# A batched matmul on one core: from a scheduled tile kernel to hand-written engine programs with a TensorE loop

## Chip, core, metric

One core of a Trainium2 chip. The metric is the device time of a whole execution in microseconds, as the median of several executions. The span, which the profile uses, runs from the first to the last instruction and is some 1.8 us shorter than the device time. Runs carry a state: fast, or slow when a run is over 1.5% above the fastest of the same kernel.

## The reference

```python
def setup_inputs():
    batch, m, k, n = 16, 512, 768, 1024
    # x: (batch, k, m), y: (batch, k, n), both float32, random

def reference(x, y):
    return np.einsum('bkm,bkn->bmn', x, y).astype(np.float32)
```

Sixteen products of a 512x768 by a 768x1024 matrix. The inputs are 75.5 MB, the output 33.55 MB, all in HBM and all float32. The kernels multiply in bf16.

## The kernel before

For each batch, SyncE issues the load of x, the load of y and, four batches late, the store of a result, all on one queue. VectorE casts x in one piece and y in two halves of K. TensorE runs four groups (mo) of 12 matmuls, and ScalarE copies each finished group out of PSUM, where the matmuls write (`ps<-y_sb,x_sb` in the page, x768). The tile framework puts in the waits. Only in the last batch is y loaded in two halves, and K is the outer loop there.

```python
    with tc.manual_schedule():
        for b in range(B):
            xs = xs_pool.tile([P, KT, M], FP32, name="xs")       # 2 buffers
            ys = ys_pool.tile([P, KT, N], FP32, name="ys")       # 2 buffers
            halves = 2 if b == B - 1 else 1
            nc.sync.dma_start(xs[:], x_v[b])
            for h in range(halves):
                ks = slice(h * KT // halves, (h + 1) * KT // halves)
                nc.sync.dma_start(ys[:, ks], y_v[b, :, ks])
            if b >= LAG:                                         # LAG = 4
                store(b - LAG)
            # ... cut: tiles x_sb, y_sb, o_sb
            nc.vector.tensor_copy(x_sb[:], xs[:])
            for h in range(2):
                ks = slice(h * KH, (h + 1) * KH)
                nc.vector.tensor_copy(y_sb[:, ks], ys[:, ks])
            for h in range(halves):
                for mo in range(MT):
                    # ... cut: matmuls over nt and this half's kt into ps[mo]
                    if h == halves - 1:
                        nc.scalar.copy(o_sb[:, mo]..., ps[mo][:])
        for b in sorted(o_tiles):
            store(b)
```

## Time and profile before

| | before |
|---|---|
| device time, us (3 runs) | 262.01 (261.9 to 262.17) |
| span of the profiled run, us | 260.4 |
| TensorE, VectorE, ScalarE busy | 73%, 32%, 25% |
| DMA queue, share of 16 engines' span | 98.5% |
| first load issued, us | 0.73 |
| last store issued and landed, us | 246.0 and 259.5 |

Two more views matter for what follows. The first is SyncE's timeline of the kernel before, with start, duration, line and the transfer:

```profile
0.73 0.38 SPq L59 DMA_DIRECT2D xs<-in_x_dram  x1
...
9.10 0.33 SPq L59 DMA_DIRECT2D xs<-in_x_dram  x1
18.07 0.33 SPq L62 DMA_DIRECT2D ys<-in_y_dram  x1
```

x of batch 2 is issued at 9.10, when the cast of x(0) is over (7.31 + 1.76 = 9.07); y of batch 2 waits until 18.07, for the casts of y(0) (14.62 + 3.43 = 18.05). The second is the view of the output tile. Its last line gives the times from issue to landing of the 16 stores, and the last store is the shortest of them:

```profile
DMA to landing us min/median/max: 13.5/32.6/36.5
```

It is issued at 246.02, when the last copy ends (244.99 + 1.01).

### The profile page before, as it was taken

To read this page: it belongs to the slowest core of one execution; us is meant where nothing else is said; L and a number is where in the kernel's file an instruction comes from. 1 tells how busy PE (TensorE), PEld (TensorE's weight loads), DVE (VectorE), ACT (ScalarE), POOL (GpSimd) and SP (SyncE) were. 2 spreads that over 40 slices of the span, in tenths; PEclk is the share of its full clock that TensorE was granted. 3 is DMA by queue.
4 is the path that set the end of the run, shared out by engine and by line. 5 is a ranking of instruction groups with operands and counts; after the bars stand their busy time and mean duration, and the time that the engine had idled before them with its cause. 6 is when DMAs were issued, how large, how long until landed. Compare 5 with 4: busy or idle time off the path is not lost.

```text
span 260.4 us, 1815 instructions
## 1 busy us (share of the span) xinstructions
PE 189.9 (73%) x768; PEld 89.1 (34%) x768; DVE 83.1 (32%) x48; ACT 66.2 (25%) x65; POOL 0.2 (0%) x4
## 2 busy tenths in 40 slices
PE   0049999897939949598495956939789597899600
PEld 0014555453513514244142422514325233355200
DVE  0271734525222252322524214252132522252000
ACT  1003343433321313314033330412404114131600
POOL 0000000000000000000000000000000000000000
PEclk9999999999986997979899997997959869799955
DMA  7999999999999999999999999999999999999995
GB/s 276 430 427 425 451 420 436 423 386 421 439 428 430 422 433 445 418 435 422 435 436 414 452 405 448 429 415 452 413 434 426 421 447 416 427 437 422 428 435 214
DMA packets 7065, 109.18 MB, mean 419 GB/s; under 512 B 784, under 2 KB 784, under 8 KB 784
## 3 DMA queue, kind: packets, MB, share of 16 engines
q1 hardware_dynamic: 7056, 109.06, 98.5%
q8 instruction: 6, 0.10, 0.1%
q14 instruction: 3, 0.02, 0.0%
HBM read 75.50 MB, written 33.55 MB: 419 GB/s over the span
## 4 chain that ended last, share of the span: by engine, by line
DMA 74%; DVE 11%; PE 8%; ACT 0%; issue 0%; SPq 0%; DVEq 0%
DMA ys<-in_y_dram 74%; DVE y_sb L70 11%; PE ps L83 8%; ACT o_sb L88 0%; SPq L59 0%; DVEq L70 0%
## 5 line engine op out<-in xcount | busy, mean ns | idle before, releaser
L83 PE MATMUL ps<-y_sb,x_sb 128*128 128x512 bf16 x768 | 189.9, 410 | 55.1 <-DVE y_sb L70 55.1
L83 PEld LDWEIGHTS <-x_sb 128*128 128x128 bf16 x768 | 89.1, 118 | 155.3 <-issue 44.6
L88 ACT COPY o_sb<-ps 128x1024 f32<-128x1024 f32 x64 | 64.9, 1014 | 179.1 <-PE ps L83 179.1
L70 DVE CAST y_sb<-ys 128x3072 bf16<-128x3072 f32 x32 | 55.0, 1757 | 87.6 <-DMA ys<-in_y_dram 87.6
L67 DVE CAST x_sb<-xs 128x3072 bf16<-128x3072 f32 x16 | 28.2, 1760 | 66.4 <-DMA xs<-in_x_dram 65.6
L88 ACT ACT_TABLE_LOAD x1 | 1.3, 1283 | 0.7 <-PEq L105 0.7
L105 POOL MEMSET const-bfloat16-1.0<- 128x1 bf16 x1 | 0.1, 101 | 0.0
L105 POOL MEMSET const-uint8-127<- 128x1 uint8 x1 | 0.1, 101 | 0.0
L105 POOL MEMSET const-float32-0.0<- 128x1 f32 x1 | 0.1, 98 | 0.2 <-issue 0.2
L105 POOL MEMSET const-float32-1.0<- 128x1 f32 x1 | 0.1, 98 | 0.0
## 6 DMA issues: line engine op xcount, KB each, us to landing
ys<-in_y_dram SPq DMA_DIRECT2D x15, 3072.0 KB, 28.1
out_dram<-o_sb SPq DMA_DIRECT2D x16, 2048.0 KB, 32.6
xs<-in_x_dram SPq DMA_DIRECT2D x16, 1536.0 KB, 29.7
ys<-in_y_dram SPq DMA_DIRECT2D x2, 1536.0 KB, 26.1
```

The lines of the kernel that those rows point to most:

```text
L67: nc.vector.tensor_copy(x_sb[:], xs[:])
L70: nc.vector.tensor_copy(y_sb[:, ks], ys[:, ks])
L83: nc.tensor.matmul(ps[mo][:, nt], x_w[:, kt, mo], y_sb[:, kt, nt * NF:(nt + 1) * NF], start=(kt == 0), stop=(kt == KT - 1))
L88: nc.scalar.copy(o_sb[:, mo].rearrange("p (t f) -> p t f", f=NF), ps[mo][:])
L105: nc = _bacc.Bacc("TRN2", target_bir_lowering=False, num_devices=1)
```

## The change

Intent: replace the framework's schedule by one program per engine, with semaphores chosen by hand. TensorE's program becomes a loop over pairs of batches. It takes credits ("ready" from the casts, "room" from the copies) and subtracts them as it takes them, so that the loop body can be the same each time. Three things change with it. x is issued only after all casts of the batch two earlier. The last batch is like the others. The whole stands in a critical section with its own entry and exit.

```diff
-            halves = 2 if b == B - 1 else 1
-            nc.sync.dma_start(xs[:], x_v[b])
-            ... y in one or two loads
+    ctx.enter_context(tc.tile_critical())
+    ... buffers and semaphores by name; block = ec(nc.Block())
+    @block.sync
+    def _(sync):
+        for b in range(B):
+            if b >= 2:
+                sync.wait_ge(cast, b - 1)
+            sync.dma_start(xs[i][:], x_v[b]).then_inc(sx[i], 16)
+            sync.dma_start(ys[i][:], y_v[b]).then_inc(sy[i], 16)
+            if b >= LAG:
+                store(b - LAG)
+    @block.vector
+    ... waits on sx, sy; each cast adds 1 to ready; a drain adds 1 to cast
+    def batch(tensor, i, first):
+        tensor.wait_ge(ready, 2).then_inc(ready, -2)
+        for mo in range(MT):
+            tensor.wait_ge(room, 1).then_inc(room, -1)
+            for nt in range(NT):
+                for kt in range(KT):
+                    if mo == 0 and nt == 0 and kt == KH:
+                        tensor.wait_ge(ready, 1).then_inc(ready, -1)
+                    mm = nc.tensor.matmul(...)
+            mm.then_inc(groups, 1)
+    @block.tensor
+    def _(tensor):
+        with tensor.Fori(0, B // 2):
+            batch(tensor, 0, False)
+            batch(tensor, 1, False)
+    @block.scalar
+    ... waits on groups; each copy adds 1 to room; a drain adds 1 to outs
```

More of the change, by code (lines that the diff above doesn't have):

```diff
@@ L37 @@
     o_v = out.rearrange("b (p mo) n -> b p mo n", mo=MT)
-    xs_pool = ctx.enter_context(tc.tile_pool(name="xs_pool", bufs=2))
-    ys_pool = ctx.enter_context(tc.tile_pool(name="ys_pool", bufs=2))
-    x_pool = ctx.enter_context(tc.tile_pool(name="x_pool", bufs=2))
-    y_pool = ctx.enter_context(tc.tile_pool(name="y_pool", bufs=2))
-    o_pool = ctx.enter_context(tc.tile_pool(name="o_pool", bufs=5))
-    psum = ctx.enter_context(tc.tile_pool(name="psum", bufs=4, space=bass.MemoryType.PSUM))
@@ L45 @@
     LAG = 4
+    NO = 5
     KH = KT // 2
-    o_tiles = {}
-    def store(b):
-        o_sb = o_tiles.pop(b)
-        nc.sync.dma_start(o_v[b], o_sb[:])
-    with tc.manual_schedule():
-        for b in range(B):
-            xs = xs_pool.tile([P, KT, M], FP32, name="xs")
-            ys = ys_pool.tile([P, KT, N], FP32, name="ys")
-            halves = 2 if b == B - 1 else 1
-            nc.sync.dma_start(xs[:], x_v[b])
-            for h in range(halves):
-                ks = slice(h * KT // halves, (h + 1) * KT // halves)
-                nc.sync.dma_start(ys[:, ks], y_v[b, :, ks])
+    GP = NT * NF
@@ new lines @@
+    ctx.enter_context(tc.tile_critical())
+    ec = ctx.enter_context
+    xs = [ec(nc.sbuf_tensor(f"xs{i}", [P, KT, M], FP32)) for i in range(2)]
+    ys = [ec(nc.sbuf_tensor(f"ys{i}", [P, KT, N], FP32)) for i in range(2)]
+    xb = [ec(nc.sbuf_tensor(f"xb{i}", [P, KT, M], BF16)) for i in range(2)]
+    yb = [ec(nc.sbuf_tensor(f"yb{i}", [P, KT, N], BF16)) for i in range(2)]
+    ob = [ec(nc.sbuf_tensor(f"ob{i}", [P, MT, N], FP32)) for i in range(NO)]
+    ps = [ec(nc.psum_tensor(f"ps{i}", [P, NT, NF], FP32)) for i in range(MT)]
@@ new lines, with store @@
+    sx = [ec(nc.semaphore(f"sx{i}")) for i in range(2)]
+    sy = [ec(nc.semaphore(f"sy{i}")) for i in range(2)]
+    so = [ec(nc.semaphore(f"so{i}")) for i in range(NO)]
+    cast = ec(nc.semaphore("cast"))
+    ready = ec(nc.semaphore("ready"))
+    room = ec(nc.semaphore("room"))
+    groups = ec(nc.semaphore("groups"))
+    outs = ec(nc.semaphore("outs"))
+    block = ec(nc.Block())
+    @block.sync
+    def _(sync):
+        def store(b):
+            sync.wait_ge(outs, b + 1)
+            sync.dma_start(o_v[b], ob[b % NO][:]).then_inc(so[b % NO], 16)
+        for b in range(B):
+            i = b % 2
+            if b >= 2:
+                sync.wait_ge(cast, b - 1)
+            sync.dma_start(xs[i][:], x_v[b]).then_inc(sx[i], 16)
+            sync.dma_start(ys[i][:], y_v[b]).then_inc(sy[i], 16)
@@ L63, with _ @@
             if b >= LAG:
                 store(b - LAG)
-            x_sb = x_pool.tile([P, KT, M], BF16, name="x_sb")
-            y_sb = y_pool.tile([P, KT, N], BF16, name="y_sb")
-            nc.vector.tensor_copy(x_sb[:], xs[:])
+        for b in range(B - LAG, B):
+            store(b)
+        for i in range(NO):
+            sync.wait_ge(so[i], 16 * len(range(i, B, NO)))
+    @block.vector
+    def _(vector):
+        for b in range(B):
+            i = b % 2
+            n = 16 * (b // 2 + 1)
+            if b >= 2:
+                vector.wait_ge(groups, MT * (b - 1))
+            vector.wait_ge(sx[i], n)
+            nc.vector.tensor_copy(xb[i][:], xs[i][:]).then_inc(ready, 1)
+            vector.wait_ge(sy[i], n)
@@ L68 @@
             for h in range(2):
                 ks = slice(h * KH, (h + 1) * KH)
-                nc.vector.tensor_copy(y_sb[:, ks], ys[:, ks])
-            x_w = x_sb[:].rearrange("p k (j mo) -> p k mo j", mo=MT)
-            o_sb = o_pool.tile([P, MT, N], FP32, name="o_sb")
-            o_tiles[b] = o_sb
-            ps = {}
-            for h in range(halves):
-                for mo in range(MT):
-                    if h == 0:
-                        ps[mo] = psum.tile([P, NT, NF], FP32, name="ps")
-                    for nt in range(NT):
-                        for kt in range(h * KT // halves, (h + 1) * KT // halves):
-                            nc.tensor.matmul(
-                                ps[mo][:, nt], x_w[:, kt, mo],
-                                y_sb[:, kt, nt * NF:(nt + 1) * NF],
-                                start=(kt == 0), stop=(kt == KT - 1))
-                    if h == halves - 1:
-                        nc.scalar.copy(o_sb[:, mo].rearrange("p (t f) -> p t f", f=NF), ps[mo][:])
@@ L89 @@
-        for b in sorted(o_tiles):
-            store(b)
+                nc.vector.tensor_copy(yb[i][:, ks], ys[i][:, ks]).then_inc(ready, 1)
+            vector.drain().then_inc(cast, 1)
+    def batch(tensor, i, first):
+        x_w = xb[i][:].rearrange("p k (j mo) -> p k mo j", mo=MT)
+        tensor.wait_ge(ready, 2).then_inc(ready, -2)
[5 more added lines that the diff above has]
+                        tensor.wait_ge(ready, 1).then_inc(ready, -1)
+                    mm = nc.tensor.matmul(
+                        ps[mo][:, nt], x_w[:, kt, mo],
+                        yb[i][:, kt, nt * NF:(nt + 1) * NF],
+                        start=(kt == 0), stop=(kt == KT - 1))
+            mm.then_inc(groups, 1)
@@ new lines, in _ @@
+    @block.tensor
[4 more added lines that the diff above has]
+    @block.scalar
+    def _(scalar):
+        nc.scalar.nop().then_inc(room, MT)
+        for b in range(B):
+            for mo in range(MT):
+                if mo == 0 and b >= NO:
+                    scalar.wait_ge(so[b % NO], 16 * (b // NO))
+                scalar.wait_ge(groups, MT * b + mo + 1)
+                nc.scalar.copy(ob[b % NO][:, mo].rearrange("p (t f) -> p t f", f=NF),
+                               ps[mo][:]).then_inc(room, 1)
+            scalar.drain().then_inc(outs, 1)
```

## The prediction

> **What bounds the kernel now.** I read the page's slices first, then its queues, its groups, the timelines of TensorE and VectorE, and last the stretches at the end.
>
> ```profile
> DMA  7999999999999999999999999999999999999995
> ...
> q1 hardware_dynamic: 7056, 109.06, 98.5%
> q8 instruction: 6, 0.10, 0.1%
> ...
> DMA 74%; DVE 11%; PE 8%; ACT 0%; issue 0%; SPq 0%; DVEq 0%
> ...
> L83 PE MATMUL ps<-y_sb,x_sb 128*128 128x512 bf16 x768 | 189.9, 410 | 55.1 <-DVE y_sb L70 55.1
> L88 ACT COPY o_sb<-ps 128x1024 f32<-128x1024 f32 x64 | 64.9, 1014 | 179.1 <-PE ps L83 179.1
> L70 DVE CAST y_sb<-ys 128x3072 bf16<-128x3072 f32 x32 | 55.0, 1757 | 87.6 <-DMA ys<-in_y_dram 87.6
> ```
>
> The transfer engines are full in every slice but the first and the last; one queue carries 109.06 MB. Every compute engine idles for their sake: the casts 87.6 us for y, TensorE 55.1 us for the casts. The chain's 74% on DMA says the same. Its 8% of PE is the last 22 us of matmul, so the end wants a closer look.
>
> The stretches show how flat this is (columns: stretch, its length, busy time and count of PE, PEld, DVE, ACT, POOL, then clock, DMA share, GB/s):
>
> ```profile
> 3.00:256.00 253.00, 189.88 (x768) 89.12 (x768) 83.11 (x48) 64.91 (x64) 0.00 (x0) 0.90 1.01 429
> ...
> 256.00:260.40 4.40, 0.00 (x0) 0.00 (x0) 0.00 (x0) 0.00 (x0) 0.00 (x0) 0.50 0.26 112
> ```
>
> For 253 us the queue never runs dry, at 429 GB/s. What is left to win is the 3 us ahead and the 4.4 us behind. A batch moves 1.57 MB of x, 3.15 of y and 2.10 of output, 6.8 MB, so 15.9 us at that rate; the casts of y repeat every 15.8 to 16.1 us in VectorE's timeline. TensorE needs 10.9 to 13.5 us for a batch (the same view cut by batch), so it has 2.4 to 5 us to spare in each.
>
> [...] a y load takes 28.1 us from issue to landing though its own bytes need 7.3. So an issue that comes late costs nothing while the queue still holds work. [...]
>
> **The change, part by part.**
>
> Issue order. Both kernels issue x(b), y(b), store(b-4) on one queue, so the bytes stand in the same order. Only x(b) is issued later: it waited for the cast of x(b-2), now for both casts of y(b-2) as well. In the timeline of before, x of batch 2 went out at 9.10 us and its y at 18.07; now both go at about 18.1. Is the queue then dry? y(0) was seen at 14.6, and behind it stood x(1) and y(1), 4.7 MB or 11 us, so until about 25.6 (where y(1) is seen). An issue at 18.1 is 7.5 us early. In the steady part one or two stores of 4.9 us stand there too. Cost: 0.
>
> TensorE. 768 pairs of weight load and matmul written out become one loop body of 96 pairs run 8 times; the built pairs are the same instructions. A batch gets six waits (two on casts, four on freed accumulators) and half a loop branch. I have no measured duration for these; [...] Against 2.4 to 5 us to spare: 0 on the path. The credit for an accumulator is given by the same copy that was waited for before. VectorE and ScalarE get a drain per batch, where they idle 10 us. The instruction packets shrink with the program, at most 0.10 MB, or -0.2 us.
>
> Start and end. The hand-written part has its own entry and exit[...]. I put 0.3 us at the start and 0.6 us at the end, an estimate from the end of before, where 0.9 us lie between the landing of the last store (246.02 + 13.5 = 259.5) and the end at 260.4. Together +0.9 us.
>
> The last batch. Before, y(15) came in two halves and TensorE did the first half of K for all four groups while the second was under way. Now it is one load, and TensorE runs whole groups.
>
> ```profile
> 223.03 21.92 PE L83 MATMUL ps<-y_sb,x_sb 128*128 128x512 bf16 x93 [0.82 <-DVE y_sb L70]
> ```
> ```profile
> 231.77 1.76 DVE L70 CAST y_sb<-ys 128x3072 bf16<-128x3072 f32 x1 [1.90 <-DMA ys<-in_y_dram]
> 235.35 1.76 DVE L70 CAST y_sb<-ys 128x3072 bf16<-128x3072 f32 x1 [1.82 <-DMA ys<-in_y_dram]
> ```
> ```profile
> 244.99 1.01 ACT L88 COPY o_sb<-ps 128x1024 f32<-128x1024 f32 x1 [0.28 <-PE ps L83]
> ```
>
> Before, 93 matmuls ran in one piece to 244.95, though y(15) was only complete at 235.35. After, the whole y is still complete at 235.35; first cast done 237.1, second 238.9; the first three matmuls go between, the other 45 take 9.9 us (full clock) to 12.7 us (slowest batch in the timeline), say 11.3. That ends at 250.2; the copy (1.01) and the drain give 251.3. The last store was issued at 246.02, so it slips by 5.3 us (3.9 to 6.7).
>
> How much of that shows? Before, that store took 13.5 us to land. Its 2.10 MB need 4.9 us at 429, and the fixed part is about 2.9 us, from the first x load: issued 0.73, used at 7.31, 6.6 us for 1.57 MB that need 3.7. So it lay 5.7 us behind stores 11 to 14. A slip of 5.3 is just covered; 6.7 would show 1.0. I book 0.3 us.
>
> Sum: 262.0 + 0 (issue) + 0 (TensorE) - 0.2 (instruction bytes) + 0.9 (entry, exit) + 0.3 (last batch) = 263.0 us.
>
> **The rivals.**
>
> First: the queue runs dry because x is issued late. For it: SyncE now has one gate a batch and issues x and y together. Against: the 7.5 us of bytes still queued at the earliest, tightest place, more later. If dry for 1 us in each of 14 batches, 276 us; I give it 3%.
>
> Second: TensorE becomes the bound. For it: the waits now stand in its own stream and stop its sequencer, so weight loads may not be pulled ahead[...]. From 18 to 52 us TensorE runs without a pause even before. Against: it would have to lose more than 2.4 to 5 us per batch, every batch. If every weight load (118 ns) were exposed, 48 x 118 = 5.7 us, it would run at 17 to 18 us a batch and the time would be some 280 to 290. I give it 3%.
>
> Third: the tail shows more. If the queue's lead over the last store is less than my 5.7 us, or the clock stays low after the new pause, the whole slip less a few us shows: 264 to 267. For it: the granted clock falls to half in the last slices, and the lead is a difference of three numbers. I give it 25%.
>
> Fourth: faster. Engine programs without the framework's bookkeeping may start and stop sooner. But even with the first 3 us and the last 4.4 halved the gain is 3.7 us, 1.4%; over 2% it can hardly be.
>
> **Range and chances.** The middle part is pinned by bytes, so the spread comes from the ends: -1.5 us if entry and exit are shorter than before, +2.8 us if the tail shows in part. Predicted 263.0, range 261.2 to 265.8. Faster by over 2% (under 256.8): 0.02. Slower (over 267.2): 0.06, from rivals one and two and the worst of three. Within 2%: 0.92.
>
> **What would show it.** Issue order right: every slice of DMA at 9 from the second to the last but one, about 429 GB/s, time to landing of x shorter by up to 9 us while y's stays near 28. TensorE right: 768 matmuls, 11 to 14 us per batch, its idle time still put down to the casts. Last batch right: last copy ends at 250 to 253, the last store lands in about 8 us instead of 13.5, bandwidth without a hole before it. A hole of over 1 us between the fourth and the fifth of the last stores would show the third rival; an idle DMA slice in the middle the first; ScalarE's copies spaced wider than 2.6 us at full clock, the second. Entry and exit: the first issue later than 0.73, and more than 0.9 us after the last landing. The prediction is wrong if the time leaves 261 to 266, or if it is met with a DMA share under 98%.

That the waits and the loop's branch would not fill TensorE's 2.4 to 5 us to spare was the estimate, with nothing measured for either. That the 429 GB/s of the middle would not rise was not shown beforehand. For entry and exit there is only the estimate from the end of before. That transfers come in in the order of their issue is what the start of before shows: x(0), y(0), x(1) and y(1), issued in this order, are taken up by the casts at 7.31, 14.62, 18.31 and 25.62 us. The clock beside the two figures for 45 matmuls: those from 52.05 took 9.87 us at a granted clock of 1.00, those from 207.22 took 12.70 us at 0.77.

## The result, and the profile after

The changed kernel took 263.03 us (262.92 to 263.22, 4 runs); the kernel before took 262.0 beside it. Ratios in this document are the mean time of one kernel's runs over the mean of the other's in the same rounds. They leave out the first run of each kernel, so they are not quite the ratio of the medians quoted. Here the ratio is 1.0039, with a 95% interval of 1.0022 to 1.0057: the same within 2%, and slower by 1 us. The result is correct.

From the page of the changed kernel, the rows that answer to those shown of before (slices, queues, chain, groups):

```profile
DMA  7999999999999999999999999999999999999993
...
q1 hardware_dynamic: 6912, 109.05, 98.1%
q8 instruction: 1, 0.02, 0.0%
...
PE 5%; ACT 0%; issue 0%
...
L105 PE MATMUL ps<-yb,xb 128*128 128x512 bf16 x768 | 188.0, 406 | 61.6 <-PEq L100 55.9
L125 ACT COPY ob<-ps 128x1024 f32<-128x1024 f32 x64 | 64.9, 1013 | 183.6 <-PE ps L105 183.6
L93 DVE CAST yb<-ys 128x3072 bf16<-128x3072 f32 x32 | 54.9, 1757 | 88.4 <-DMA ys<-in_y_dram 88.4
```

The queue is as full as before, and the same bytes go through it. Two rows read differently, and that is an effect of the view. TensorE's 61.6 us of idle time are now put down to its own sequencer (PEq L100 55.9, L104 5.3) and no longer to the cast (DVE y_sb L70 55.1 of before): the wait is now an instruction of its own in TensorE's program. (L100 is the wait for "room", the last instruction ahead of the matmul. What TensorE waits for is "ready", L98 just before it: the last batch starts at 237.66, after the cast that ends at 235.57 + 1.76 = 237.33, while the last copy before it ended at 235.9.) The chain that ended last breaks off after 5%, at 237.62, where the last batch follows that wait (74% of it was DMA before). It does not mean that DMA left the path. The stretches show this (same columns as in the prediction):

```profile
3.00:256.00 253.00, 188.05 (x768) 87.08 (x768) 83.03 (x48) 64.86 (x64) 0.00 (x0) 0.92 1.01 429
256.00:261.20 5.20, 0.00 (x0) 0.00 (x0) 0.00 (x0) 0.00 (x0) 0.00 (x0) 0.50 0.14 60
```

The rate is 429 GB/s over the same 253 us, to the digit. All of the difference must be at the ends. SyncE's timeline of the changed kernel:

```profile
0.94 0.38 SPq L72 DMA_DIRECT2D xs<-in_x_dram  x1
...
18.49 0.33 SPq L72 DMA_DIRECT2D xs<-in_x_dram  x1
18.86 0.43 SPq L73 DMA_DIRECT2D ys<-in_y_dram  x1
```

The first load is issued 0.21 us later, which is put down to the entry. x(2) now goes out at 18.49 instead of 9.10, together with y(2). The last casts, the last matmuls and the last copy, each from its engine's timeline:

```profile
235.57 3.43 DVE L93 CAST yb<-ys 128x3072 bf16<-128x3072 f32 x2 [5.46 <-DMA ys<-in_y_dram]
```
```profile
237.66 12.01 PE L105 MATMUL ps<-yb,xb 128*128 128x512 bf16 x48 [2.79 <-PEq L100]
```
```profile
249.71 1.01 ACT L125 COPY ob<-ps 128x1024 f32<-128x1024 f32 x1 [1.58 <-PE ps L105]
```

y(15) is there at 235.57 (before: 235.35), and TensorE starts on it at 237.66, after a pause of 2.79 us that it did not have before. The last copy ends at 250.7, and the last store goes out at 250.8, which is 4.8 us later than before. The times to landing, from the view of the output tile:

```profile
DMA to landing us min/median/max: 9.0/32.1/36.5
```

It lands after 9.0 us instead of 13.5, at 259.8: 0.3 us later than before, of which 0.2 were lost at the start. So the slip of 4.8 us vanished in the queue. The end of the span follows 1.4 us after the landing instead of 0.9. The other profiles agree: both framework kernels (before, before_whole) issue their first load at 0.73 and end 0.8 to 0.9 us after the last landing; ten of the hand-written ones end 1.4 to 1.5 us after it (late_issue was not read for this), and all but two_frames issue their first load at 0.94 or 0.95.

### The profile page after: what moved, and what is told of

It is laid out like the page before. It is cut to its first block, busy times and chain, and to the rows that moved or that the text cites. A ratio compares the mean times of both kernels' runs of the same rounds, so it can differ in the third digit from the quotient of the medians.

```text
span 261.2 us, 1938 instructions
## 1 busy us (share of the span) xinstructions
PE 188.0 (72%) x768; PEld 87.1 (33%) x768; DVE 83.0 (32%) x48; ACT 66.1 (25%) x65; POOL 0.2 (0%) x4
## 5 line engine op out<-in xcount | busy, mean ns | idle before, releaser
L105 PE MATMUL ps<-yb,xb 128*128 128x512 bf16 x768 | 188.0, 406 | 61.6 <-PEq L100 55.9
L105 PEld LDWEIGHTS ps<-yb,xb 128*128 128x128 bf16 x768 | 87.1, 116 | 162.1 <-issue 96.7
L125 ACT COPY ob<-ps 128x1024 f32<-128x1024 f32 x64 | 64.9, 1013 | 183.6 <-PE ps L105 183.6
L93 DVE CAST yb<-ys 128x3072 bf16<-128x3072 f32 x32 | 54.9, 1757 | 88.4 <-DMA ys<-in_y_dram 88.4
L89 DVE CAST xb<-xs 128x3072 bf16<-128x3072 f32 x16 | 28.2, 1760 | 67.5 <-DMA xs<-in_x_dram 66.8
## 6 DMA issues: line engine op xcount, KB each, us to landing
xs<-in_x_dram SPq DMA_DIRECT2D x16, 1536.0 KB, 20.8
```

Of the source, the lines that this page charges most:

```text
L89: nc.vector.tensor_copy(xb[i][:], xs[i][:]).then_inc(ready, 1)
L93: nc.vector.tensor_copy(yb[i][:, ks], ys[i][:, ks]).then_inc(ready, 1)
L105: mm = nc.tensor.matmul(ps[mo][:, nt], x_w[:, kt, mo], yb[i][:, kt, nt * NF:(nt + 1) * NF], start=(kt == 0), stop=(kt == KT - 1))
L125: nc.scalar.copy(ob[b % NO][:, mo].rearrange("p (t f) -> p t f", f=NF), ps[mo][:]).then_inc(room, 1)
```

## The experiments

Theory: the queue of transfers sets the time; the new waits, the loop, the later issue of x and the later last store are hidden; what shows is the entry and the exit. Rivals: the tail, the loop, or the issue order makes the loss.

### The last batch alone: before_whole and last_halves

```diff
 before_whole, against the kernel before
-            halves = 2 if b == B - 1 else 1
+            halves = 1
 last_halves, against the changed kernel
-        with tensor.Fori(0, B // 2):
+        with tensor.Fori(0, B // 2 - 1):
             batch(tensor, 0, False)
             batch(tensor, 1, False)
+        batch(tensor, 0, False)
+        ... batch 15 with K halves outermost; its y in two loads, each with a semaphore
```

> The kernel before with y(15) loaded whole and the last batch run group by group: the last part of the change alone. Theory (slip of the last store covered by the queue): last store issued 4 to 6 us later than 246.0, landing time down from 13.5 to about 8 to 9 us, time within 0.4 us of before (262.0 to 262.4). Rival (the tail is the whole loss): 262.8 to 263.2.

> The changed kernel with the last batch in two halves of K again and the two y halves loaded apart. Theory (entry and exit are the loss, the tail costs nothing): last store issued near 246.3 instead of 250.8 and landing after 13.3 us, time 262.8 to 263.1, the same as the changed kernel. Rival (the tail is the loss): back at 262.0 to 262.3.

before_whole took 262.12 us beside 262.29 for before, ratio 0.9993 (0.998 to 1.0006). Its last store went out at 249.9 us and landed in 9.7, somewhat more than the 8 to 9 expected. last_halves took 263.04, ratio 1.0037 (1.0024 to 1.005). Its last copy and its stores' landing times:

```profile
244.85 1.01 ACT L147 COPY ob<-ps 128x1024 f32<-128x1024 f32 x1 [0.28 <-PE ps L132]
```
```profile
DMA to landing us min/median/max: 13.9/32.2/36.1
```

Issued at 245.9, the last store lands at 259.8, just where the changed kernel's landed, though that one was issued 4.9 us later. Doing this part alone costs nothing and undoing it gains nothing. The tail is not the loss, and the split of the last batch was not worth anything in the kernel before either.

### How much cover the tail has: late_store3 and late_store6

```diff
+    waste = ec(nc.sbuf_tensor("waste", [P, n, NT, NF], BF16))      # n = 3 or 6
 ...
+            if b == B - 1:
+                for k in range(n):
+                    nc.scalar.copy(waste[:, k], ps[MT - 1][:])
             scalar.drain().then_inc(outs, 1)
```

> The changed kernel with three needless copies of about 1.0 us each on ScalarE ahead of the release of the last store. It measures how much cover is left. Theory: the store that landed in 9.0 us needs 7.8 uncovered, so 1.2 us of cover is left: issued at 253.9, landing in 7.8, time up by 1.8 to 264.9. Rival A (no cover was left, the tail already shows): up by the full 3.0 to 266.1. Rival B (several us of cover left): within 0.3 of 263.0.

> The changed kernel with six needless copies ahead of the last store, 0.95 us each as measured with three. With three the store went out at 253.0 and landed in 6.9 us, less than the 7.8 that was reckoned to be uncovered. Theory (6.9 or a little less is the uncovered time, the cover ends near 252.9): issued at 256 to 256.6, landing in 6.3 to 6.9, time 265.8 to 266.8. Rival (the cover is not yet used up at 253): landing under 6 us, time under 265.3.

late_store3 missed its number: 263.93 us, ratio 1.0063, 0.9 above the changed kernel and not 1.8. Its runs fall apart, three between 263.2 and 263.7 and three between 264.2 and 264.4. In the profiled one (263.22) the store went out at 253.03, landed in 6.9 and was late by only 0.1 us. late_store6 met its time, 266.48 us, ratio 1.0174, and its landing; the store went out at 257.06, later than the 256 to 256.6 expected. Stores to landing in it:

```profile
DMA to landing us min/median/max: 6.3/32.2/36.5
```

Cut into stretches of one microsecond, the queue of late_store6 shows the hole that the others do not have:

```profile
253.00:254.00 1.00, 0.00 (x0) 0.00 (x0) 0.00 (x0) 1.00 (x2) 0.00 (x0) 0.50 0.08 33
254.00:255.00 1.00, 0.00 (x0) 0.00 (x0) 0.00 (x0) 1.00 (x2) 0.00 (x0) 0.50 0.00 0
...
257.00:258.00 1.00, 0.00 (x0) 0.00 (x0) 0.00 (x0) 0.01 (x1) 0.00 (x0) 0.50 0.54 229
```

A store of 2.10 MB with nothing ahead of it lands in 6.3 us. As the last store ordinarily lands at 259.8 in the changed kernel, it may go out as late as 259.8 - 6.3 = 253.5 at no cost. The check: late_store6 issued at 257.06, 3.6 us past that edge, and lost 266.48 - 262.90 = 3.6 us against the changed kernel of the same rounds. As the edge is taken from this run's own landing time, this checks only that past the edge a microsecond of delay costs one. late_store3's profiled run sits half a microsecond ahead of the edge, but it had a short last batch: its last copy into the output began at 249.22, in the changed kernel at 249.71 and in unrolled_again, whose last batch is the same program text, at 250.86. With a last batch like that of unrolled_again its store would go out at about 254.7 and cost 1.2 us, which is where the upper cluster lies. That is an estimate from these traces; only one of late_store3's runs has a profile, so the reason for the clusters is not shown.

### The entry and exit: two_frames

```diff
+    with tc.tile_critical():
+        with nc.Block() as early:
+            ... one nop on each of SyncE, TensorE, VectorE, ScalarE
     ctx.enter_context(tc.tile_critical())
```

> The changed kernel with a second, empty hand-written part (its entry, one idle instruction per engine, its exit) ahead of the real one. It doubles the suspected cost. Theory (entry plus exit cost 0.7 to 0.9 us): first load issued at 1.6 to 1.9 us instead of 0.94, time 263.7 to 264.0. Rival (the frame is free, the loss is the tail or the loop): first load at about 1.0, time 263.0 to 263.1.

It took 264.34 us, ratio 1.0077 (1.0064 to 1.009), which is 1.3 us above last_halves in the same rounds. The first load, from SyncE's timeline:

```profile
2.04 0.38 SPq L90 DMA_DIRECT2D xs<-in_x_dram  x1
```

That is 1.10 us later than in the changed kernel; the end still follows the last landing (261.2) by 1.4 us. So the frame is not free, and it shifts everything behind it. The numbers were missed (first load 1.6 to 1.9, time 263.7 to 264.0): an empty frame costs 1.3 us, more than the 0.7 that entry (0.21) and exit (0.5) of the real one show. No run takes the frame away from the hand-written kernel, so the 0.7 rests on the traces.

### The loop alone: unrolled, unrolled_again, after_again

```diff
-        with tensor.Fori(0, B // 2):
+        for _ in range(B // 2):
             batch(tensor, 0, False)
             batch(tensor, 1, False)
```

> The changed kernel with TensorE's loop written out as 16 batches, waits kept: the loop alone undone. Theory (the loop is off the path): instruction packets back to about six, 0.10 MB, time 263.0 to 263.3, TensorE's restart after a cast unchanged at about 0.3 us. Rival (the backward branch costs on the path): faster by 0.3 us or more, 262.4 to 262.7.

> The changed kernel once more, unaltered, as the control for the written-out loop. Both theories: 263.0, ratio to before 1.003 to 1.004.

> The changed kernel with TensorE's loop written out, again, now with the changed kernel beside it. The first time it was 0.4 us faster, which theory (loop off the path) did not expect. Chance: 262.9 to 263.1, and y(15) cast at 235.4 or later. A real gain of the written-out form: 262.4 to 262.8 again, y(15) cast near 234.9.

The first run took 262.63 us, ratio 1.0025 (1.0011 to 1.0039), 0.4 under the changed kernel of an earlier round. That would have spoken for the rival, so it was run again with the changed kernel beside it: 262.81 (262.6 to 263.06) against 262.90 (262.65 to 263.27), ratios to before 1.0039 and 1.0044. The intervals lie on each other. But this is no clean answer: 262.81 lies between the two bands that were set for the repeat (262.9 to 263.1 for chance, 262.4 to 262.8 for a gain), and so does y(15)'s cast, at 235.17 (234.91 in the first run). In six profiled kernels with the loop (after, after_again, early_x, extra_group, late_store3, late_store6) it is at 235.41 to 235.74; in before_whole, which has no loop either, at 235.49. In the first rounds early_x and extra_group, both with a loop, had means of 263.0 us against 262.7 for unrolled. So a cost of the loop of some 0.3 us is neither shown nor excluded. The instruction packets went from 1 back to 6, as expected.

### The issue order: early_x and late_issue

```diff
 early_x
-                sync.wait_ge(cast, b - 1)
+                sync.wait_ge(castx, b - 1)        # raised after the cast of x alone
             sync.dma_start(xs[i][:], x_v[b]).then_inc(sx[i], 16)
+            if b >= 2:
+                sync.wait_ge(cast, b - 1)
             sync.dma_start(ys[i][:], y_v[b]).then_inc(sy[i], 16)
 late_issue
                 sync.wait_ge(cast, b - 1)
+                sync.wait_ge(groups, MT * (b - 1))
```

> The changed kernel with x(b) issued as soon as the cast of x(b-2) is over, as before, y(b) after the casts of y(b-2): the issue order alone undone. Theory (the queue is never dry): x lands in about 29.7 us instead of 20.8, time unchanged, 262.9 to 263.2. Rival (late issue costs something): 262.0 to 262.5.

> The changed kernel with the loads of batch b held back until TensorE is done with batch b-2, some 10 to 12 us later than now. It looks for the edge of the 7.5 us lead. Theory (7.5 us to spare at the tightest place, x(2), and 4.9 us more for each store queued later): at x(2) issue at about 29 instead of 18.5 while the queue ends near 25.6, so a hole of about 4 us, a second of some us at x(3), smaller ones or none once stores stand in the queue; time up by 4 to 12 us. Rival A (there is much more lead than bytes in the queue tell): unchanged. Rival B (the queue is nearly dry all along): some 10 us in each of 14 batches, over 350.

early_x took 262.94 us, ratio 1.0034 (1.002 to 1.0048). Its x lands in 29.7 us again instead of 20.8; x(2) goes out at 9.34 instead of 18.49. Nine microseconds of earlier issue per batch bought nothing.

late_issue took 278.05, 280.32 and 281.56 us in its fast runs; a fourth, of 282.8, was slow. The median (280.94) and ratio (1.0741) come out only with the slow run counted in; the fast runs alone have a mean of 280.0, 1.07 times before. It is the one experiment that empties the queue in the middle, and the number was missed: 15 to 18.5 us over the changed kernel, and not 4 to 12. The stretches in its profile (the run of 278.05):

```profile
24.00:26.00 2.00, 2.00 (x11) 1.02 (x10) 0.35 (x1) 0.88 (x1) 0.00 (x0) 1.00 0.23 98
26.00:28.00 2.00, 2.00 (x11) 1.03 (x10) 2.00 (x2) 1.02 (x1) 0.00 (x0) 1.00 0.00 0
28.00:30.00 2.00, 2.00 (x11) 1.08 (x10) 1.08 (x1) 0.95 (x1) 0.00 (x0) 1.00 0.00 0
...
54.00:56.00 2.00, 2.00 (x11) 1.03 (x10) 0.64 (x1) 1.01 (x1) 0.00 (x0) 1.00 0.03 12
```

The first hole is at the expected place, from about 24.5 to 30 us. The second, from 53 to 60, is longer, not shorter: the first hole made TensorE wait for y(2) until 46, and that delay held back the issue of x(4) and y(4) to 59.25. Smaller dips follow up to 75 us. From there on, with stores in the queue, it stays full. Taken as one stretch, from 24 to 76 us, the queue moved 302 GB/s; from 76 to 271 us it was 429 again. The gap is worth 52 x (1 - 302/429) = 15.4 us, the whole loss of this run (15.0). Why the other fast runs lost up to 3.5 us more is not shown. So the lead is real, but it was reckoned too long: the queue ran dry at about 24.5, 6 us after the changed kernel's issue at 18.5, and not 7.5. The reckoning took the time at which VectorE saw y(1), 25.6, for the end of the bytes. How a delay feeds the next one I had not reckoned either.

### TensorE's spare time: extra_group

```diff
+                    if again and mo == 1:          # the first 14 batches
+                        ... the six matmuls of this accumulation once more (both nt)
             mm.then_inc(groups, 1)
```

> The changed kernel with 12 needless matmuls (one accumulation again, 2.6 us at full clock) in each of the first 14 batches, on purpose. Theory (TensorE has 2.4 to 5 us to spare in a batch): the early stretch without pauses grows by up to 2.6 us a batch but the queue stays full; time within 0.5 us of the changed kernel, 263.0 to 263.5. Rival (the waits have eaten TensorE's spare time): 2.6 us in each of 14 batches, up to 299.

The edit also takes the last two batches out of the loop. It took 263.0 us, ratio 1.0032 (1.0017 to 1.0047). In its stretches of one batch:

```profile
64.00:79.90 15.90, 15.90 (x76) 8.33 (x74) 5.23 (x4) 4.55 (x5) 0.00 (x0) 1.00 1.01 433
...
112.00:127.80 15.80, 13.28 (x60) 6.64 (x60) 5.03 (x4) 4.05 (x4) 0.00 (x0) 1.00 1.00 422
```

A quarter more matmuls per batch, TensorE without a pause up to about 110 us, and the time doesn't move. TensorE's spare time is there, after all waits and the loop are paid.

## Why the prediction was right

The time was forecast at 263.0 us and came to 263.03, which owes something to luck: the +0.3 for the last batch was wrong, the -0.2 for instruction bytes was not found, and the two nearly cancel.

**What binds** held. 429 GB/s over the same 253 us in both kernels.

**Issue order, 0 us**: shown by early_x. The lead was 6 us and not 7.5, as late_issue shows; that changes nothing here.

**TensorE, 0 us on the path**: for the waits, shown by extra_group; for the loop, the unrolled pair leaves up to 0.3 us open. While the credits are already there, no cost of them shows even on TensorE. The first twelve copies of ScalarE, before and then after, follow three batches of matmuls with one turn of the loop in them:

```profile
22.07 1.02 ACT L88 COPY o_sb<-ps 128x1024 f32<-128x1024 f32 x1 [20.06 <-PE ps L83]
...
50.56 1.01 ACT L88 COPY o_sb<-ps 128x1024 f32<-128x1024 f32 x1 [1.58 <-PE ps L83]
```
```profile
22.41 1.01 ACT L125 COPY ob<-ps 128x1024 f32<-128x1024 f32 x1 [20.15 <-PE ps L105]
...
50.90 1.01 ACT L125 COPY ob<-ps 128x1024 f32<-128x1024 f32 x1 [1.57 <-PE ps L105]
```

Both take 28.49 us, and in both the copies are 2.59 us apart throughout, so no cost of the turn shows. Where TensorE has to wait for a cast, it restarts later: 0.33 us after the first cast of y (237.33 to 237.66; it was 0.05 before, 16.38 to 16.43), with two wait instructions in between, and 0.14 us after the second (239.00 to 239.14; 0.05 before, 18.05 to 18.10), with one. The growth of TensorE's idle time, 61.6 - 55.1 = 6.5 us, is not the cost of the waits: 4.7 us of it come from the last batch's later end (244.95 to 249.67) and 1.8 from shorter busy time (189.88 to 188.05).

**Instruction bytes, -0.2 us**: not found. The bytes did go, from 0.10 to 0.02 MB, but writing the loop out again, which brings the six packets back, cost no time (262.81 against 262.90; if anything it gained). The runs of one kernel scatter by more than 0.2 us.

**Entry and exit, +0.9 us**: the first issue is 0.21 us later and the end lies 0.5 us further behind the last landing, together 0.7 of the 1.0 us between the medians (0.8 between the profiled spans). two_frames shows that such a frame costs time on the path: 1.3 us for the empty one. The remaining 0.1 to 0.3 us are not attributed; the loop may have a part in them, and runs of one kernel scatter by as much.

**Last batch, +0.3 us**: the mechanism was right, the term was mis-sized. The last store slipped by 4.8 us (5.3 forecast), and it cost 0: before_whole and last_halves both say so. The step that failed is "the fixed part is about 2.9 us", taken from the first load. A late store with an empty queue has 6.3 - 4.9 = 1.4 us of it. The first load ran while the queue was still getting up to speed (86, 184 and 344 GB/s in the second, third and fourth microsecond of before), with y(0) queued right behind it, and its end was taken when the cast began; which of these made the 2.9 is not separated. So the last store of before lay 13.5 - 6.3 = 7.2 us behind the others, not 5.7, and the slip was covered with room to spare.

Of the rivals, the third had the most weight (25%). It would have needed 2.7 us more of slip. Of the second, one thing did come about: in the kernel before the first weight load runs at 9.13, long ahead of its matmul at 16.43, and in the changed kernel at 17.01, just ahead of its matmul at 17.05. The copies stand 2.59 us apart in both all the same.

## What to carry to other kernels

When the transfer engines are full from end to end, as here at 429 GB/s for 253 us, ask of each changed wait only whether it empties the queue: count the bytes still queued ahead of the transfer at the moment of its late issue. Nine microseconds of later issue, a quarter more matmuls and 4.8 us of later last store cost nothing here. Once the lead was used up, a later last store cost a microsecond for each microsecond (3.6 for 3.6). What does show is what lies ahead of the first transfer and behind the last: the frame of the hand-written part cost about 0.7 us there, and neither the earlier issue of x nor the halved last batch earned it back (early_x 262.94, last_halves 263.04 us, the changed kernel 263.03).
